# Left operands made five products ahead, and a row of 1/rms spread one product sooner, in a hybrid decoder layer

## The chip, the cores and the metric

The kernel runs on one core of a Trainium2 chip. The metric is the time of one execution on the device in microseconds; the median of three runs is taken. TensorE does the matrix products (PE in the profile, its weight loads PEld), VectorE (DVE) the elementwise work on two inputs, ScalarE (ACT) copies and functions of one input, GpSimd (POOL) here little but issuing the DMAs that add to what lies at their target, and SyncE (SP) issues the plain DMAs.

## The reference, cut to what matters

One decoder layer on 1024 positions of width 1024, in float32:

```python
h = rms_norm(x, g_mix)
va, ga, xb, gb, sa, sb = split(h @ w_in + b_in)
y_a = silu(layer_norm(conv31(va * sigmoid(ga)))) @ w_a_out
y_b = (rg_lru(conv4(xb)) * gelu(gb)) @ w_b_out
x   = x + (sigmoid(sa) * y_a + sigmoid(sb) * y_b) @ w_o     # x1 below
h   = rms_norm(x, g_mlp)
x   = x + square(relu(h @ w_1)) @ w_2                       # up and down products
out = rms_norm(x, g_final)
```

The change lies at the passage from the product with `w_o`, which makes x1, over the norm of x1 to the first products with `w_1`.

## The kernel before

**Products in two parts.** Each float32 operand is split into a high part, rounded to the fast matmul format, and a low part, the rest; a product is then high*high + high*low + low*high. The high part is a copy on ScalarE. The low part is made either on VectorE (`low`, line 1062: source minus high part) or with a DMA (`split_dma`, lines 63 to 67): ScalarE writes the negated, rounded source (line 65), GpSimd issues a DMA that adds the source to it (line 66), and ScalarE writes the high part (line 67). Which sign is kept where does not matter here: a product of this kind can run its first two matmuls as soon as line 67 is done, and its third only once that DMA has landed.

**Blocks of seven products.** The products with `w_a_out` ("a"), `w_o` ("o") and `w_1` ("u") are cut two by two and done with seven block products in place of eight. One block product is twelve matmuls of 128x128 by 128x512 (`g_mm`, line 1266; `up_mm`, line 1544), four pieces of the inner dimension by three pairs of parts. The sequence of these products is a list, `gseq` (line 1197): 28 for "a", 28 for "o", and then eight of "u", the block products 1 and 2 of the first four pairs of output blocks. So index 51 is the last of the four "o" products number 5, 52 to 55 are the four "o" products number 3, 56 to 59 are ("u", 0 to 3, 1) and 60 to 63 are ("u", 0 to 3, 2). In the profile the results of "o" are called go0a, go3e and the like, by pair and bank, and those of "u" gu0a to gu3a. The rest of the products with `w_1` follow in a second list, `useq` (line 1717), with results f0b, f0c, f0d and so on; its left operands are made by `up_lhs` (line 1510) and are called o, from sums and differences s of the raw weights.

**The order is written by hand.** The order on every engine in this part is the program's. The loop over `gseq` does, for each step n: the work after product n-1 (`g_post`), the twelve matmuls of product n, the left operand of a product further on (`g_lhs`, line 1249), the sums that a still later operand needs, and then a list of extra steps from a table `GX`:

```python
for n in range(len(gseq) + 1):                                  # 1701
    ...
    g_get(n - 1, g_post)                                        # 1703
    if n == o0 + 22:
        x1_root(0)                                              # 1705
    ...
    g_get(n, g_mm)                                              # 1711
    g_get(n + 4, g_lhs)                                         # 1712
    g_get(n + 5, g_sums)
    for f, *a in GX.get(n, ()):                                 # 1714
        f(*a)
```

`o0` is 28, so the entry 22 of the second table is step 50. `u0` is 56. For "u", `g_lhs` always goes by `split_dma`, with the raw weights (`raws`, in the profile w_raw) as source; they are loaded by `up_load` (line 1500) in steps 44 to 50. In the profile the operand of a "u" product in `gseq` is called gu as well, and its split shows as ACT L65 and ACT L67 with gu<-w_raw and its DMA as POOL L66 gu<-w_raw.

**The norm of x1.** The positions are kept in two halves, even and odd tokens. For the even ones: squares and their sums by column (steps 42 to 49), the root (`x1_root`, line 1434), four diagonal blocks with 1/rms on the diagonal, made in turn by VectorE and ScalarE (`x1_diag`, lines 1453 and 1455, tile rdm), and four matmuls with a block of ones, which spread 1/rms over all partitions (`x1_spread`, line 1458, tile rbm):

```python
def x1_spread(o):                                               # 1458
    rd, rbk[o] = rbk[o], bank(f"rbm{o}")
    for i in range(4):
        d = slice(i * P, (i + 1) * P)
        nc.tensor.matmul(rbk[o][:, d], ones, rd[:, d], start=True, stop=True)
```

Then VectorE scales x1 (`x1_normed`, line 1468), and `g_parts` (line 1208) makes the two parts of the right operands: gu1h and gu1l for block product 1, gu2h and gu2l for number 2. The even tokens' 1/rms is spread in step 51, behind product 51. For the odd tokens the transposition on TensorE, the squares of the eight transposed banks on ScalarE (`x1_rows`, line 1404, squares at line 1418) and the root stand in step 56, the diagonal blocks in step 57 and the spread in step 58. Before that, `x1_turn` (line 1385) writes the even tokens' x1 to memory with sixteen DMAs on SyncE's queue, ahead of two more loads of raw weights.

The result banks in PSUM are eight, the large SBUF tiles 37 (`T`, line 44), handed out in the order in which they become free.

Of the kernel before, what the change touches and what calls it, by code (L numbers as in the profile page):

```python
# [30 lines left out]
def trunk_kernel(ctx: ExitStack, tc: tile.TileContext, x, xt_in, xt_eo, vecs, w_in, w_a_out, w_b_out,  # L31
# [668 lines left out]
    def vector_work(end):  # L700
        for ready, _, cost, f, a in sorted(todo, key=lambda x: x[:2]):
            dve(cost, ready, f, *a)
        todo.clear()
        taps["wait"] += fresh
        fresh.clear()
        fill(end)
# [77 lines left out]
    for i in range(2, NZ):  # L784
        n = zseq.index((i, 1))
# [281 lines left out]
    def b_load(j):  # L1067
        for n in range(2):
            braw[j, n] = W(f"wb{j}{n}_raw", "raw").rearrange("p (k c) -> p k c", c=P)
            nc.sync.dma_start(braw[j, n], w_b_out[j, n])  # L1070

    def b_parts(j):
        bw[j] = []
        for n in range(2):
            raw = braw.pop((j, n))
            h, l = (W(f"wb{j}{n}_{x}", "w" + x, F32R).rearrange("p (k c) -> p k c", c=P) for x in "hl")
            nc.scalar.activation(h, raw, AF.Copy)
            later(at("A", 0.8), 0.92, low, l, raw, h)
            bw[j] += [(h[:, k, :], l[:, k, :]) for k in range(6)]

    def b_gate(j):
        for hf in range(2):
            sb[j, hf] = EV(f"sb{j}{hf}").rearrange("p (o n) -> p o n", o=2)
            nc.sync.dma_start(sb[j, hf], halved(spill[1, j], hf))

    def b_mm(j):
        bps[j] = ps = [bank(f"yb{j}{hf}") for hf in range(2)]
        ops = [(w, wl, *hg[k]) for k, (w, wl) in enumerate(bw.pop(j))]
        if j < 7:
            todo = [x for w, wl, h, l in ops for x in ((w, h), (w, l))]  # L1090
            todo += [(wl, h) for w, wl, h, l in ops]
        else:

            todo = [x for w, wl, h, l in ops for x in ((w, h), (w, l), (wl, h))]
        for n, (a, b) in enumerate(todo):
            for hf in range(2):
                nc.tensor.matmul(ps[hf], a, b[:, HALVES[hf]], start=n == 0, stop=n == len(todo) - 1)  # L1097
        at("P", 72 * MM)

    def b_out(j):  # L1100
        ps = bps.pop(j)
        for hf in range(2):
            def mult(g, src, j, hf):
                tt(g, src.rearrange("p (n o) -> p o n", o=2), g, ALU.mult)
                nc.sync.dma_start(halved(mbd[j], hf), g)

            later(0, 0.63, mult, sb.pop((j, hf)), ps[hf], j, hf)
# [4 lines left out]
    def n_load():  # L1112
        for o in range(2):
            for kk in range(2):
                for c2 in range(2):
                    q[kk, o, c2] = a = T(f"q{kk}{o}{c2}")
                    for i in range(2):
                        nc.sync.dma_start(a[:, HALVES[i]], yd[4 * kk + 2 * c2 + i, :, HALVES[o]])
# [23 lines left out]
    def n_mean():  # L1142
        for o in range(2):
            mean[o] = n_sum(ysum[0][:, HALVES[o]], f"mu{o}")

    def n_center(o):
        held = []

        def add(s):
            tt(vacc[o], vacc[o], s, ALU.add)  # L1150

        for kk, c2, i in n_pieces(o):
            a = q[kk, o, c2][:, HALVES[i]]
            dve(0.63, 0, tt, a, a, mean[o], ALU.subtract)
            s = EV(f"sq{o}{kk}{c2}{i}")
            if o not in vacc:
                vacc[o] = s
                nc.scalar.activation(s, a, AF.Square)
                at("A", 0.62, clk["V"])
                continue  # L1160
            nc.scalar.activation(s, a, AF.Square)
            ready = at("A", 0.62, clk["V"])
            if held:
                dve(0.63, held[0][0], add, held.pop(0)[1])
            held.append((ready, s))
        dve(0.63, held[0][0], add, held[0][1])

    def n_var(o):
        rstd[o] = n_sum(vacc[o], f"var{o}")

    def n_root(o):
        pv = rstd[o]
        v, s, r = EV(f"lv{o}"), EV(f"lsd{o}"), EV(f"lr{o}")
        nc.vector.tensor_scalar(v, pv, EPS, None, ALU.add)
        newton_rstd(r, v, s, s)
        at("V", 7.5)
        at("A", 1.9)
        rstd[o] = r

    def n_scale(kk, o):  # L1180
        for c2 in range(2):
            for i in range(2):
                a, j = q[kk, o, c2][:, HALVES[i]], 4 * kk + 2 * c2 + i
                dve(0.63, 0, tt, a, a, rstd[o], ALU.mult)
                nc.scalar.activation(a, a, AF.Silu, scale=lng_c[:, j:j + 1], bias=lnb_c[:, j:j + 1])
                at("A", 0.62, clk["V"])
# [10 lines left out]
    gseq = [(w, i, p) for w in "ao" for p in GORD for i in range(GP)]  # L1197
# [10 lines left out]
    def g_parts(w, p, c2):  # L1208
        src = g_src(w, p, c2)
        gh[w, p, c2] = h = T(f"g{w}{p}h{c2}", F32R)  # L1210
        gl[w, p, c2] = l = T(f"g{w}{p}l{c2}", F32R)
        if w == "u" and p == 2:
            split_dma(src, h, l)
            at("A", 2.0)
            return
        nc.scalar.activation(h, src, AF.Copy)
        later(at("A", 1.0), 1.2, low, l, src, h)
# [12 lines left out]
    def g_load(w, i, kk):  # L1230
        graw[w, i, kk] = raw = T(f"w{w}{i}_{kk}").rearrange("p (m k c) -> p m k c", m=2, c=P)
        nc.sync.dma_start(raw, g_left[w][2 * i:2 * i + 2, :, 4 * kk:4 * kk + 4, :].rearrange(
            "m p k c -> p m k c"))
# [377 lines left out]
    def g_get(n, f):  # L1611
        return f(*gseq[n]) if 0 <= n < len(gseq) else None
# [23 lines left out]
        19: ((x1_add,), (x1_sq, 2, 1), (up_load, 3, (0,))),  # L1636
        20: ((x1_add,), (x1_sq, 3, 1), (flush,), (x1_turn, 0)),
        21: ((x1_add,), (flush,), (x1_cols,), (x1_turn, 1), (up_load, 0, (1,))),
        22: ((x1_diag, 0), (up_load, 1, (1,))),
        23: ((x1_spread, 0), (x1_normed, 0, 0)), 24: ((g_parts, "u", 1, 0), (g_parts, "u", 1, 1)),  # L1640
        25: ((x1_normed, 1, 0),), 26: ((g_parts, "u", 2, 0),), 27: ((g_parts, "u", 2, 1),)}.items()})
    u0 = 2 * o0
    GX.update({u0 + n: v for n, v in {
# [6 lines left out]
    with tc.manual_schedule(engines=ENGINES):  # L1650
        for j in range(8):
            clk["A"], clk["V"] = max(clk["A"], clk["P"] + 0.5), max(clk["V"], clk["P"] - 2)
            if j == 0:
                b_load(1)
                b_gate(0)
                n_load()
            if j == 2:
                n_mean()
            if j == 4:
                n_var(0)  # L1660
                n_var(1)
            if j:
                b_out(j - 1)
            b_gate(j + 1) if j < 7 else None
            b_mm(j)
            if j < 7:
                b_parts(j + 1)
            if j < 6:
                b_load(j + 2)
            vector_work(clk["V"])  # L1670
            if j < 2:
                vector_work(math.inf if j else clk["P"] - 0.3)
            elif j < 4:
                n_center(j - 2)
            elif j == 4:
                n_root(0)
                n_root(1)
            elif j == 5:
                for b in (0, 1, 3, 2):
                    n_scale(b % 2, b // 2)  # L1680
            elif j == 6:
                g_parts("a", 1, 0)
                g_parts("a", 1, 1)
                g_load("a", 0, 0)
                g_load("a", 1, 0)
            else:
                g_load("a", 2, 0)
                g_get(0, g_lhs)
                g_load("a", 3, 0)
                g_get(1, g_lhs)  # L1690
                g_t("a", 0, 1, 2)
                g_t("a", 1, 1, 2)
                g_parts("a", 2, 0)
                g_get(2, g_lhs)
                g_parts("a", 2, 1)
                g_load("a", 0, 1)
                g_get(3, g_lhs)
                g_load("a", 1, 1)
            vector_work(clk["V"])
        b_out(7)  # L1700
        for n in range(len(gseq) + 1):
            clk["A"], clk["V"] = max(clk["A"], clk["P"] + 0.5), max(clk["V"], clk["P"] - 2)
            g_get(n - 1, g_post)
            if n == o0 + 22:
                x1_root(0)
            if n > o0:
                vector_work(clk["V"])
                if n == u0:
                    to_mlp()
            g_get(n + 3, g_gate)  # L1710
            g_get(n, g_mm)
            g_get(n + 4, g_lhs)
            g_get(n + 5, g_sums)
            for f, *a in GX.get(n, ()):
                f(*a)
            vector_work(clk["P"] - 0.3)
# [382 lines left out]
```

## Time and profile before

| what | value |
|---|---|
| median of 3 runs | 1544.23 us (1544.19 to 1544.71) |
| profiled execution | 1544.64 us, its span 1542.9 us |
| TensorE busy | 1533.1 us, 99% of the span, 6782 instructions |
| VectorE busy | 1222.5 us (79%) |
| ScalarE busy | 903.6 us (59%) |
| GpSimd busy | 184.4 us (12%) |
| granted TensorE clock | 0.999 |
| DMA | 307.82 MB, 200 GB/s on average |

The profile is of one execution. Times in it count from the start of the span. A row of a timeline gives the start, the duration, the engine, the line, the operation, the tiles (out<-in, without their numbers), how many instructions were merged into the row, and in brackets the idle time just before and what ended it. Matmuls overlap: a duration of 0.39 goes with a start every 0.227. In the rows of DMA issues the last number is the time from issue to landing in microseconds. The shares of the queues q0 (GpSimd's DMAs) and q1 (SyncE's) are of all 16 DMA engines in the window asked for.

### The profile page before, as it was taken

What the parts mean: (1) busy time and instruction counts of PE and PEld (TensorE: products, weight loads), DVE (VectorE), ACT (ScalarE), POOL (GpSimd) and SP (SyncE); (2) the same over time, 40 slices, a digit from 0 to 9 for tenths busy, and PEclk for the clock granted to TensorE, in tenths of its full rate; (3) what the DMA queues carried; (4) which work ended last, traced back from release to release, by engine and by line L of the source; (5) the groups of instructions that cost most, each with busy time, mean ns of one, the idle gap of its engine ahead of it and who ended that gap; (6) DMA issues with size and microseconds to landing.
All of it is one profiled execution on the core that took longest, in us unless ns stands there. A gap on an engine that the chain in (4) does not pass through costs nothing.

```text
span 1542.9 us, 19178 instructions
## 1 busy us (share of the span) xinstructions
PE 1533.1 (99%) x6782; PEld 1262.4 (82%) x6782; DVE 1222.5 (79%) x1648; ACT 903.6 (59%) x1261; POOL 184.4 (12%) x219
## 2 busy tenths in 40 slices
PE   9999999999999999999999999999999999999998
PEld 8888788888888888888888887888888888888886
DVE  6899999979899997478569879755555558888897
ACT  6648576567567667345275777554444475555553
POOL 0000000002222222000022332000000001111110
PEclk9999999999999999999999999999999999999999
DMA  8776978898997879953579898333333779888862
GB/s 347 197 189 161 251 187 222 217 280 217 247 253 196 193 191 246 327 157 116 182 201 299 197 193 204 137 122 112 113 114 111 241 216 228 223 222 224 209 130 110
DMA packets 132288, 307.82 MB, mean 200 GB/s; under 512 B 13232, under 2 KB 35248, under 8 KB 132192
## 3 DMA queue, kind: packets, MB, share of 16 engines
q1 hardware_dynamic: 101744, 230.60, 46.0%
q0 software_dynamic: 30304, 75.74, 26.9%
q8 instruction: 53, 0.87, 0.2%
q14 instruction: 43, 0.35, 0.1%
q10 hardware_dynamic: 144, 0.26, 0.0%
HBM read 147.69 MB, written 58.72 MB: 134 GB/s over the span
## 4 chain that ended last, share of the span: by engine, by line
PE 95%; DMA 2%; issue 1%; DVE 1%; SPq 0%; POOL 0%; ACT 0%; POOLq 0%; DVEq 0%
PE z L726 18%; PE d L1863 15%; PE yb L1097 8%; PE e L1983 3%; PE keep L1863 2%; PE z L258 1%; PE rg L534 1%; PE rg L536 1%; PE rg L535 1%; DMA x<-in_x_dram 1%; DMA gu<-w_raw 1%; DMA xc<-in_xt_dram 0%; PE go3f L1274 0%; PE f15d L1550 0%; PE f15c L1550 0%
## 5 line engine op out<-in xcount | busy, mean ns | idle before, releaser
L726 PE MATMUL z<-xh,win_h 128*128 128x512 f32 x400 | 124.9, 390 | 0.0
L726 PE MATMUL z<-xl,win_h 128*128 128x512 f32 x400 | 124.5, 389 | 0.0
L1875 DVE TENSOR_TENSOR acc<-acc,d 128x1024 f32<-128x1024 f32 x72 | 87.8, 1219 | 33.3 <-PE d L1863 32.6
L726 PE MATMUL z<-xh,win_l 128*128 128x512 f32 x400 | 98.2, 391 | 0.0
L726 PEld LDWEIGHTS z<-xh,win_l 128*128 128x128 f32 x400 | 75.1, 188 | 16.9
L726 PEld LDWEIGHTS z<-xh,win_h 128*128 128x128 f32 x400 | 75.0, 188 | 16.7 <-ACT win_h L67 0.7
L637 DVE SCALAR_TENSOR_TENSOR y<-u,vec,y 128x511 f32<-128x511 f32 (+14 forms) x120 | 88.3, 736 | 0.0
L726 PEld LDWEIGHTS z<-xl,win_h 128*128 128x128 f32 x400 | 75.1, 188 | 15.8
L542 ACT ACTIVATE g<-rg,vec 96x1024 f32<-96x1024 f32 x32 | 35.6, 1113 | 85.5 <-issue 46.0
L637 DVE SCALAR_TENSOR_TENSOR y<-yt,csum,y 128x511 f32<-128x511 f32 (+6 forms) x112 | 82.5, 736 | 0.0
L637 DVE SCALAR_TENSOR_TENSOR yt<-u,vec,yt 128x511 f32<-128x511 f32 (+6 forms) x112 | 82.5, 736 | 0.0
L66 POOL DMA_DIRECT2D win_l<-win_raw x25 | 21.8, 871 | 324.3 <-ACT win_l L65 312.3
L1538 ACT ACTIVATE o<-s 128x512 fp32r<-128x512 f32 x56 | 33.7, 623 | 45.7 <-DVE s L1522 26.4
L66 POOL DMA_DIRECT2D zo<-zw x42 | 36.6, 871 | 129.4 <-ACT zo L65 116.1
L1097 PE MATMUL yb<-hgl,wb_h 128*128 128x512 f32 x168 | 51.7, 389 | 0.0
L1097 PE MATMUL yb<-hgh,wb_h 128*128 128x512 f32 x168 | 51.7, 389 | 0.0
L486 DVE SCALAR_TENSOR_TENSOR v<-xb,vec,v 128x1023 f32<-128x1023 f32 (+2 forms) x36 | 46.2, 1282 | 6.9 <-ACT v L477 6.1
L66 POOL DMA_DIRECT2D db_1l<-wr x7 | 6.1, 870 | 310.5 <-ACT db_1l L65 287.9
L1097 PE MATMUL yb<-hgh,wb_l 128*128 128x512 f32 x168 | 41.0, 389 | 0.0
L65 ACT ACTIVATE zo<-zw 128x512 fp32r<-128x512 f32 x42 | 26.3, 625 | 20.7 <-PE z10f L914 2.1
L1063 DVE TENSOR_TENSOR o<-s,o 128x512 fp32r<-128x512 f32 x56 | 37.3, 683 | 0.5 <-ACT o L1538 0.5
L1097 PEld LDWEIGHTS yb<-hgh,wb_h 128*128 128x128 f32 x168 | 31.5, 188 | 6.6
(1805 smaller groups left out, 4669.7 us busy)
## 6 DMA issues: line engine op xcount, KB each, us to landing
w_raw<-in_w_dram SPq DMA_DIRECT2D x34, 512.0 KB, 5.7
fr<-fd SPq DMA_DIRECT2D x32, 512.0 KB, 6.3
wr<-in_w_dram SPq DMA_DIRECT2D x32, 512.0 KB, 6.6
zw<-in_w_in_dram SPq DMA_DIRECT2D x28, 512.0 KB, 6.3
win_raw<-in_w_in_dram SPq DMA_DIRECT2D x25, 512.0 KB, 6.8
win_l<-win_raw POOLq DMA_DIRECT2D x25, 512.0 KB, 6.7
zo<-zw POOLq DMA_DIRECT2D x42, 256.0 KB, 5.6
gates<-zg SPq DMA_DIRECT2D x32, 256.0 KB, 3.9
```

What stands on the lines that cost most here:

```text
L65: nc.scalar.activation(l, src, AF.Copy, scale=-1.0)
L66: nc.gpsimd.dma_start(l, src, accum_op=ALU.add)
L486: nc.vector.scalar_tensor_tensor(v[:, d:S], a[:, 0:S - d], cbw_c[:, w * 12 + t:w * 12 + t + 1], v[:, d:S], ALU.mult, ALU.add)
L542: nc.scalar.activation(a, gps.pop((n, gi))[:HD, :], AF.Sigmoid, bias=(ba_c, bx_c)[gi][:, n:n + 1])
L637: nc.vector.scalar_tensor_tensor(o[:, k:], a[:, 0:HS - k], c, o[:, k:], ALU.mult, add)
L726: nc.tensor.matmul(zps[s][:, HALVES[hf]], w[:, k, :], xw[k][part][hf], start=n == 0, stop=n == 23)
L1063: tt(l, src, h.bitcast(F32), ALU.subtract)
L1097: nc.tensor.matmul(ps[hf], a, b[:, HALVES[hf]], start=n == 0, stop=n == len(todo) - 1)
L1538: nc.scalar.activation(o[:, 0], src, AF.Copy)
L1863: nc.tensor.matmul(o, a, b, start=n == 0 and (p != 1 or g == 0), stop=n == len(todo) - 1, skip_group_check=p == 1 and g > 0)
L1875: tt(acc[p, q2], acc[p, q2], ps, ALU.add)
L1983: nc.tensor.matmul(o, a, b, start=n == 0 and t not in LOADED, stop=n == len(todo) - 1, skip_group_check=t in LOADED)
```

## The change

Two things are moved; no instruction is added or taken away.

The left operands of the eight "u" products in `gseq` are made five products ahead, where those of all others are still made four ahead. In step 51 two operands are made, those of products 55 and 56; from then on step n makes that of product n+5, and step 59 makes none. Since the call stands ahead of the table's extra steps, the operand of product 61, for one, now is split in step 56 ahead of `up_lhs` and `x1_rows`, in place of step 57 behind them; that of 57 is split in step 52 ahead of `g_parts` of gu1.

The four matmuls that spread the even tokens' 1/rms stand in step 50, behind product 50 and directly behind `x1_diag`, in place of step 51, behind product 51. The scaling of x1 that reads them stays in the table of step 51.

```diff
-        22: ((x1_diag, 0), (up_load, 1, (1,))),
-        23: ((x1_spread, 0), (x1_normed, 0, 0)), 24: ((g_parts, "u", 1, 0), (g_parts, "u", 1, 1)),
+        22: ((x1_diag, 0), (x1_spread, 0), (up_load, 1, (1,))),
+        23: ((x1_normed, 0, 0),), 24: ((g_parts, "u", 1, 0), (g_parts, "u", 1, 1)),
...
             g_get(n, g_mm)
-            g_get(n + 4, g_lhs)
+
+            for d in (4, 5):
+                if n + d < len(gseq) and (gseq[n + d][0] == "u") == (d == 5):
+                    g_get(n + d, g_lhs)
             g_get(n + 5, g_sums)
```

## The prediction

> **What bounds the kernel now.** I read the page first, then the waits of TensorE, then the timelines of all engines around the one wait that the change can touch, and last the DMA view, one issue at a time, for the time from issue to landing.
>
> ```profile
> span 1542.9 us, 19178 instructions
> ...
> PE 95%; DMA 2%; issue 1%; DVE 1%; SPq 0%; POOL 0%; ACT 0%; POOLq 0%; DVEq 0%
> ...
> PE gu1a L1274 <- DMA gu<-w_raw: 1.7, 1, 1.7
> ```
>
> The chain that ended last is matmul for 95% of the span, and between the start-up and the end the waits view holds one wait of TensorE: the second half product of pair 1 (gu1a) waits once for a DMA. So the kernel is a row of matmuls, and whatever does not move a matmul is free. All else that the change does has to be read by one question: which transfer or vector result does TensorE meet late, or just in time?
>
> ```profile
> 932.95 0.39 PE L1274 MATMUL gu1a<-gu2h,gu 128*128 128x512 f32 x1
> 933.17 0.39 PE L1274 MATMUL gu1a<-gu2l,gu 128*128 128x512 f32 x1
> 935.23 0.74 PE L1274 MATMUL gu1a<-gu2h,gu 128*128 128x512 f32 x2 [1.67 <-DMA gu<-w_raw]
> ...
> 937.67 0.39 PE L1274 MATMUL gu2a<-gu2h,gu 128*128 128x512 f32 x1
> ```
>
> The first two matmuls need the high part of the left operand, the third its low part, which an accumulating DMA makes. Matmuls start 0.227 apart where nothing waits (932.95 to 933.17), so twelve take 2.72; this product takes 937.67 - 932.95 = 4.72. The stall costs 2.00 us, of which 0.16 is slow restart beyond the late start (935.23 against 933.40 is 1.83).
>
> **Why that transfer is late.** ScalarE, which writes the high part and the negated source (lines 65 and 67), GpSimd, which issues the accumulate, and the landing times of three transfers in the order of the queue:
>
> ```profile
> 916.64 0.61 ACT L65 ACTIVATE gu<-w_raw 128x512 fp32r<-128x512 f32 x1
> ...
> 917.68 0.62 ACT L65 ACTIVATE o<-s 128x512 fp32r<-128x512 f32 x1
> ...
> 918.72 0.57 ACT L1418 ACTIVATE sq<-tr 128x512 f32<-128x512 f32 x1
> ...
> 924.45 0.62 ACT L65 ACTIVATE gu<-w_raw 128x512 fp32r<-128x512 f32 x1
> ...
> 917.55 0.87 POOL L66 DMA_DIRECT2D gu<-w_raw  x1 [0.60 <-ACT gu L65]
> 918.59 0.87 POOL L66 DMA_DIRECT2D o<-s  x1 [0.17 <-issue]
> 925.36 0.94 POOL L66 DMA_DIRECT2D gu<-w_raw  x1 [5.90 <-ACT gu L65]
> ...
> gu<-w_raw POOLq DMA_DIRECT2D x1, 256.0 KB, 12.4
> o<-s POOLq DMA_DIRECT2D x1, 256.0 KB, 14.0
> gu<-w_raw POOLq DMA_DIRECT2D x1, 256.0 KB, 9.8
> ```
>
> In step 56 ScalarE splits the operand of product 60 (916.64), then that of product 64 (o, 917.68), then squares eight transposed banks from 918.72 on, and only in step 57, at 924.45, comes to product 61. Its DMA goes out at 925.36 and lands 9.8 later, at 935.2: that is the stall.
>
> **The change, part by part.**
>
> *Operands five ahead.* For products 56 to 63 the split moves one step earlier; step 51 does two. Nothing is added or taken away: eight pairs of ScalarE copies and eight accumulates, as before. Product 61 moves from step 57 to step 56 and so ahead of the squares: its DMA goes out before the o transfer, no later than 918.6 instead of 925.36. A pessimistic landing: it takes the place in the queue that o has now, 918.59 + 14.0 = 932.6. Needed at 933.40. The stall goes: **-2.00**. Products 62 and 63 take the ScalarE places of 61 and 62. Without the stall the low part of 62 is read 2.00 sooner than now, at 937.67 + 0.45 - 2.00 = 936.1; in 61's present place it lands, with 61's own time, at 925.36 + 9.8 = 935.2. That holds with 0.9 to spare. On ScalarE product 57 lands in front of the high parts of gu1, where the engine is idle:
>
> ```profile
> 905.68 1.06 ACT L1216 ACTIVATE gu1h<-x 128x1024 fp32r<-128x1024 f32 x1 [2.56 <-issue]
> ```
>
> One pair costs about 1.04 (two copies, 0.52 from start to start: 916.64 to 917.68 is the pair), and 2.56 covers it. Without that cover gu1's high part would come 1 us later, at some 908, and products 52 to 55, four times 2.72, still lie ahead of its first reader. On GpSimd the accumulates move ahead of those of gu2 only; SyncE's own order is untouched.
>
> *The spread one product sooner.* Four small matmuls move from behind product 51 to behind product 50, so TensorE, which takes them in order, now meets them while their input is being made. The first product queued behind them, go3e, and everything after it waits with them.
>
> ```profile
> 900.38 0.39 PE L1274 MATMUL go3e<-go5h,go 128*128 128x512 f32 x1
> ...
> 903.10 1.05 PE L1463 MATMUL rbm<-rdm,ones 128*128 128x128 f32 x8
> 903.91 0.48 PE L1274 MATMUL go0e<-go3h,go 128*128 128x512 f32 x1
> ...
> 900.35 0.70 ACT L1455 ACTIVATE rdm<-ident,stm 128x128 f32<-128x128 f32 x2 [0.29 <-DVE stm L105]
> ...
> 900.29 0.48 DVE L1453 TENSOR_SCALAR rdm<-ident,stm 128x128 f32<-128x128 f32 x2
> ```
>
> The spread would start at 900.38 and take 0.81 (903.10 to 903.91), 0.2 for each of its four blocks. The blocks come in turn from VectorE and ScalarE, the last one at 900.35 + 0.70 = 901.05. If each matmul waits for its own block alone, the last is due at 900.99 and loses 0.06; if all wait for the last, 0.7. The first block is half of VectorE's pair, at about 900.55, so I take **+0.4**. A gain is excluded, since the matmuls are the same. What it gives VectorE (the scaling of x1 some 2 us sooner) moves nothing that TensorE waits for.
>
> *What is late next.* So far -1.6. After this point TensorE runs 1.6 us sooner against VectorE and ScalarE, whose own chains do not start sooner. The tightest meeting that follows is in f1d, product (1,7):
>
> ```profile
> 948.17 0.87 POOL L66 DMA_DIRECT2D o<-s  x1 [0.80 <-ACT o L65]
> ...
> o<-s POOLq DMA_DIRECT2D x1, 256.0 KB, 8.2
> ...
> 957.17 0.62 PE L1550 MATMUL f1d<-gu7h,o 128*128 128x512 f32 x2
> ...
> 947.24 0.63 ACT L65 ACTIVATE o<-s 128x512 fp32r<-128x512 f32 x1
> ...
> 946.51 0.69 DVE L1526 TENSOR_TENSOR s<-w_raw,w_raw 128x512 f32<-128x512 f32 x1
> ...
> 927.67 5.35 DVE L462 SCALAR_TENSOR_TENSOR x<-x,vec,rbm 128x512 f32<-128x512 f32 x8
> ```
>
> The low part lands at 948.17 + 8.2 = 956.4 and is read at 957.17: 0.8 to spare. Its source s is done on VectorE at 946.51 + 0.69 = 947.20 and split at 947.24, and VectorE works without a break worth naming from the second scaling at 927.67, behind the odd tokens' spread, up to there. So this transfer does not follow TensorE forward; the 0.4 of the early spread even pushes it back a little (I take 0.15, between 0 and 0.4). Read time falls to 955.6, landing is 956.5: a new wait of 0.95, and with the 0.16 of slow restart **+1.1**. (f0d, one product before, waits for its own part of it; that shortens the wait in f1d and adds nothing.) The next to come has more room:
>
> ```profile
> 950.16 0.87 POOL L66 DMA_DIRECT2D o<-s  x1 [1.12 <-ACT o L65]
> ...
> o<-s POOLq DMA_DIRECT2D x1, 256.0 KB, 8.0
> ```
>
> It lands at 958.2 and is read twelve matmuls after 957.17, at 959.89: 1.7 to spare, more than is left of the gain by then.
>
> Sum: -2.0 + 0.4 + 1.1 = **-0.5 us**. The profiled execution took 1544.64 (its span and 1.74 around it), so 1544.1 for such a run; the median of the runs is 0.41 lower, which makes 1543.7.
>
> A rule to weigh: the Trainium skill (DMA: Bandwidth & Descriptors, section "Anatomy of one DMA — SWDGE (gpsimd) path") fits one such transfer with 2.0 us and its bytes over 436 GB/s, which is an estimate of 2.6 us for 256 KB. The rows above (8.2 to 14.0) do not agree, and the measurement decides; by the page there would be neither the old stall nor the new wait, and the change would be worth +0.4.
>
> **The rivals.**
>
> *All of the gain stays.* The new wait stands on 8.2 us for one transfer. One of the same size and kind, three issues earlier in the same queue, has this row:
>
> ```profile
> o<-s POOLq DMA_DIRECT2D x1, 256.0 KB, 3.3
> ```
>
> If the transfers around 948 shift against the weight loads beside them so that this one takes 6 to 7, only -2.0 + 0.4 = -1.6 remains: 1542.6. Against it: its issue is tied to VectorE and the loads beside it keep their places.
>
> *The transfer is early but lands no sooner.* The DMA engines are loaded through all of this stretch; if product 61's part is overtaken by the row writes of x1 all the same, the stall stays, swallows the 0.4, and nothing changes: 1544.2. Against it: even o's present place in the queue is early enough.
>
> *Slower: the moved accumulates hold up a weight load.* Products 57 to 59 now put their transfers out near 904 to 908, beside SyncE's writes of x1 and ahead of the loads at 909.11.
>
> ```profile
> 909.11 1.71 SPq L1505 DMA_DIRECT2D w_raw<-in_w_dram  x2
> ...
> w_raw<-in_w_dram SPq DMA_DIRECT2D x1, 512.0 KB, 5.9
> w_raw<-in_w_dram SPq DMA_DIRECT2D x1, 512.0 KB, 9.4
> ...
> 915.11 0.69 DVE L462 TENSOR_TENSOR x<-xe,go3e 128x512 f32<-128x512 f32 x1 [0.90 <-PE go3e L1274]
> 915.71 0.69 DVE L1521 TENSOR_TENSOR s<-w_raw 128x512 f32<-128x512 f32 x1
> ...
> q1 hardware_dynamic: 557, 0.27, 52.1%
> ...
> q1 hardware_dynamic: 321, 0.35, 91.5%
> ```
>
> The last two rows are 908 to 910 and 910 to 912: in the second the accumulates' queue is almost empty and SyncE's gets 91.5% of the engines instead of 52.1%. Filling that gap takes this share away. The first load lands at 909.11 + 5.9 = 915.0, VectorE takes it at 915.71 (at 916.1 with the 0.4), behind it stand o's split, the squares, the odd tokens' spread and VectorE's long chain to f1d. So 1.1 us is free; what is beyond goes into that chain. If the first load took the 9.4 of the second, it would be 3.5 late, the chain 2.4 late instead of 0.15, and the sum -0.5 + 2.2 = +1.7: 1545.9. It decides from about 1.8 us of delay on.
>
> The Trainium skill (DMA: Bandwidth & Descriptors, section "Queues, rings and completion order") says that each DMA engine takes its queues in turn, packet by packet; the two shares agree with it, and it is the reason to give this rival weight.
>
> **How the numbers follow.** Two runs differ by some 0.5 us (1544.19 to 1544.71); 0.2% is 3.1 us and about what a measurement of this kernel can tell from no change. Forecast, the stall traded for a shorter one in f1d (1543.7): 0.55. All gain kept (1542.6): 0.2. Nothing moved (1544.2): 0.08. The load held up (1545 to 1546): 0.17. The range takes in the second case and the first half of the last: 1542.6 to 1545.3. Faster by over 0.2% would need more than the only stall there is: 0.01. Slower by over 0.2% would need a delay of 5 us in that load, or buffers handed out in another order that bring a stall I cannot see from here: 0.04. Within: 0.95.
>
> **What would show it.** Right: no wait of gu1a for gu<-w_raw; the accumulate of product 61 issued before 919; the first spread starting at 900.4 to 901 with a gap of 0.1 to 0.7 before go3e; and a wait of f0d or f1d for o<-s of about 1 us in all. Wrong: f0d and f1d without a wait (all gain kept), gu1a or gu2a still waiting (the queue, not the issue, decides), or the odd tokens' spread waiting for its blocks with w_raw landing after 916.5 (the slower rival).

## The result, and the profile after

The changed kernel is slower: 1550.73 us median of five runs (1549.31 to 1550.84), against 1544.23 us (1543.59 to 1544.93) of the kernel before on the same chip. The ratio is 1.0039, 95% interval 1.0024 to 1.0054. The forecast was 1543.7 us with a range up to 1545.3, so it was wrong, and on the wrong side.

The profiled execution of after took 1550.05 us. Two lines of its page, the span and the chain that ended last:

```profile
span 1548.3 us, 19179 instructions
...
PE 94%; DMA 2%; issue 2%; DVE 1%; POOL 1%; SPq 0%; ACT 0%; POOLq 0%; DVEq 0%; ACTq 0%
```

Then the waits of TensorE (us in total, times, longest):

```profile
PE tr L1413 <- DVE x1r L1422: 4.3, 1, 4.3
...
PE f0d L1550 <- DMA o<-s: 0.3, 1, 0.3
```

The kernel is still a row of matmuls. The wait of gu1a for gu<-w_raw is gone, as forecast. In its place the transposes of the odd tokens (tr) wait 4.3 us, once, for VectorE. The rows left out are of the start-up.

Now the timelines of ScalarE, VectorE and TensorE around that wait, of after:

```profile
907.19 0.63 ACT L65 ACTIVATE gu<-w_raw 128x512 fp32r<-128x512 f32 x1 [0.95 <-DMA x1d<-x1r]
...
916.24 0.63 ACT L65 ACTIVATE gu<-w_raw 128x512 fp32r<-128x512 f32 x1 [7.89 <-DMA x1d<-x1r]
...
923.16 0.61 ACT L65 ACTIVATE o<-s 128x512 fp32r<-128x512 f32 x1
...
924.20 0.57 ACT L1418 ACTIVATE sq<-tr 128x512 f32<-128x512 f32 x1
...
918.99 0.69 DVE L1521 TENSOR_TENSOR s<-w_raw 128x512 f32<-128x512 f32 x1 [2.66 <-DMA w_raw<-in_w_dram]
...
924.90 3.68 DVE L1422 COPY x1r<-tr 128x512 f32<-128x512 f32 x6 [4.49 <-ACT sq L1418]
...
918.16 3.22 PE L1413 MATMUL tr<-ident,x 128*128 128x128 f32 x28
925.65 0.66 PE L1413 MATMUL tr<-ident,x 128*128 128x128 f32 x4 [4.27 <-DVE x1r L1422]
926.24 0.60 PE L1274 MATMUL gu1a<-gu1h,gu 128*128 128x512 f32 x1
926.64 0.63 PE L1274 MATMUL gu1a<-gu1l,gu 128*128 128x512 f32 x1
...
930.69 0.39 PE L1274 MATMUL gu2a<-gu1h,gu 128*128 128x512 f32 x1
```

Read it from the bottom up. 28 of the 32 transposes run; the last four have no PSUM bank, because VectorE has not yet copied one out. VectorE's copies (L1422) wait for ScalarE's squares, which start at 924.20; in before they started at 918.72. The squares stand in ScalarE's queue behind everything else, and ScalarE lost 7.89 us at 916.24: the split of product 59's operand waits for a write of x1 to memory (x1d<-x1r). The tile that this split fills had been given the SBUF buffer of the last turned piece of x1, and SyncE's DMA was still reading from it. In before the same buffer went to the operand of product 60, at 916.64, and the write had landed by then. (The trace leaves buffer numbers out; which tile takes over which buffer stands in the program as built.) So one product further ahead, plus an order of hand-outs shifted by one, put ScalarE in front of a buffer that was not free. The wait of 0.95 at 907.19 is the same thing one piece of x1 earlier: product 58's operand has the buffer of the last but one.

The DMA view of after, the issues between 905 and 917 (KB each, median us from issue to landing):

```profile
w_raw<-in_w_dram SPq DMA_DIRECT2D x2, 512.0 KB, 9.5
gu<-w_raw POOLq DMA_DIRECT2D x2, 256.0 KB, 8.0
x1d<-x1r SPq DMA_DIRECT2D x3, 128.0 KB, 8.7
```

The same issues in before:

```profile
w_raw<-in_w_dram SPq DMA_DIRECT2D x2, 512.0 KB, 7.7
...
x1d<-x1r SPq DMA_DIRECT2D x3, 128.0 KB, 6.4
```

The last write of x1 alone, first its issue on SyncE's queue and its landing in after, then its landing in before:

```profile
907.46 1.68 SPq L1394 DMA_DIRECT2D x1d<-x1r  x1
...
x1d<-x1r SPq DMA_DIRECT2D x1, 128.0 KB, 8.7
...
x1d<-x1r SPq DMA_DIRECT2D x1, 128.0 KB, 6.1
```

And the shares of the queues in after, for 908 to 910 and, the last row, 910 to 912 (in before SyncE's q1 had 52.1% and 91.5%):

```profile
q0 software_dynamic: 172, 0.31, 92.4%
q1 hardware_dynamic: 134, 0.06, 15.9%
...
q1 hardware_dynamic: 454, 0.22, 46.0%
```

The accumulates of products 57 and 58, issued at 904.26 and 908.12 in place of 909.02 and behind it, took SyncE's share of the DMA engines, as the slower rival said: 15.9% and 46.0% are left. (That of product 59 went out only at 917.16, behind the wait.) The writes of x1 land after 8.7 us in place of 6.4. The last one, at 907.46 + 8.7 = 916.2, is what ends ScalarE's wait. But the late landing is the smaller part of that wait: ScalarE wanted the buffer at 916.24 - 7.89 = 908.35, and with the 6.1 us of before it would have come free at 913.6, so an estimated 5.2 of the 7.89 us come from the order of the hand-outs alone. The weight load, issued behind the writes, is late too: VectorE waits 2.66 us for it at 918.99. In this trace that holds up nothing: the sum is done at 920.4, and ScalarE comes to its split at 923.16.

One more view, the stretches of TensorE in after with the clock granted (the column after the busy time):

```profile
921.40:925.60 4.20, 0.00 (x0) 1.00 1.08 194
...
926.20:930.60 4.40, 4.40 (x13) 0.61 1.07 234
```

After the idle 4.2 us TensorE gets a mean of 0.61 of its clock for the next 4.4 us. Matmuls that start 0.227 apart elsewhere start 0.40 apart here (926.24 to 926.64), and the twelve of gu1a take 4.45 in place of 2.82. The stall is thus paid nearly one and a half times.

**The sum of the two traces.** The eight matmuls of the column sums, before anything of the change, in before:

```profile
L1400 PE MATMUL cs<-ones,sq x8: 164/250/250, 896.7 to 897.4; 128*128 128x1 f32 x8
```

and in after (start of the first and of the last):

```profile
L1400 PE MATMUL cs<-ones,sq x8: 164/250/250, 896.9 to 897.6; 128*128 128x1 f32 x8
```

And TensorE's timeline of before at the places named below:

```profile
917.63 3.65 PE L1413 MATMUL tr<-ident,x 128*128 128x128 f32 x32
921.04 0.48 PE L1274 MATMUL gu1a<-gu1h,gu 128*128 128x512 f32 x1
...
923.86 0.39 PE L1274 MATMUL gu2a<-gu1h,gu 128*128 128x512 f32 x1
...
959.43 0.39 PE L1550 MATMUL f0c<-gu3h,o 128*128 128x512 f32 x1
```

After comes into the passage 0.2 later, before anything of the change. Up to the transposes it loses 0.3 more (918.16 against 917.63, less that 0.2), which is the early spread. From there to the start of gu2a it takes 930.69 - 918.16 = 12.53 where before took 923.86 - 917.63 = 6.23: 6.30 lost, of which 4.27 is the wait, 1.63 the slow clock (gu1a takes 4.45 in place of 2.82) and 0.40 the restart around it. From gu2a to f0c (964.85 in after) it gains 1.41: the 2.00 of the old stall less 0.6 that f0d and its neighbours give back. 0.2 + 0.3 + 6.3 - 1.4 = 5.4, the difference of the spans (1548.3 - 1542.9). The medians differ by 6.5; the profiled run of after was one of its faster ones, that of before lies 0.4 above its median.

### The profile page after: what moved, and what is told of

Read it like the earlier page. It is cut to its first block, busy times and chain, and to the rows that moved or that the text cites. A ratio compares the mean times of both kernels' runs of the same rounds, so it can differ in the third digit from the quotient of the medians.

```text
span 1548.3 us, 19179 instructions
## 1 busy us (share of the span) xinstructions
PE 1534.6 (99%) x6782; PEld 1262.0 (82%) x6782; DVE 1223.1 (79%) x1648; ACT 903.6 (58%) x1261; POOL 184.8 (12%) x219
## 4 chain that ended last, share of the span: by engine, by line
PE 94%; DMA 2%; issue 2%; DVE 1%; POOL 1%; SPq 0%; ACT 0%; POOLq 0%; DVEq 0%; ACTq 0%
PE z L726 18%; PE d L1866 15%; PE yb L1097 8%; PE e L1986 3%; PE keep L1866 2%; PE z L258 1%; PE rg L534 1%; PE rg L536 1%; PE rg L535 1%; DMA x<-in_x_dram 1%; DMA x1d<-x1r 1%; DMA o<-s 0%; DMA xc<-in_xt_dram 0%; PE go3f L1274 0%; PE f1d L1550 0%
## 5 line engine op out<-in xcount | busy, mean ns | idle before, releaser
L1097 PEld LDWEIGHTS yb<-hgl,wb_h 128*128 128x128 f32 x168 | 31.5, 188 | 6.6
```

## The experiments

Two theories stood after this reading. *Buffer*: the wait for the buffer of x1 is the whole cost. *Sharing*: what the moved accumulates take from SyncE's queue is the cost, through the writes of x1 and through the weight load, and the buffer is only where it shows. The early spread had to be priced by itself. The ratios below are to the kernel before as measured again beside each group: 1544.12 for the first four kernels, 1544.02 for the four with early loads that follow, 1543.96 for the last four.

**The two halves alone.** First the spread one product sooner with the operands four ahead as before:

```diff
-            for d in (4, 5):
-                if n + d < len(gseq) and (gseq[n + d][0] == "u") == (d == 5):
-                    g_get(n + d, g_lhs)
+            g_get(n + 4, g_lhs)
```

> The spread one product sooner alone, the operands four ahead as before. Theory of the early spread alone: it costs 0.5 us on TensorE (its wait for the diagonal blocks), which the old stall of gu1a swallows, so 1544.2 to 1544.7 and squares at line 1418 starting at 918.7 as before. Buffer theory: with the spread moved, the buffers of the turned x1 (x1r) are handed out again two to four operands sooner; here gu2l0, not the operand of product 59, gets the last of them. ScalarE then waits at line 65 for gu2l until that write lands, about 913.3 in place of a start at 909.8, its queue runs 1.5 us behind the old one, the squares start near 920.2, and the time is 1545.5 to 1546.5, with no w_raw later than 915.5. Sharing theory (moved accumulates slow the weight load): nothing was moved there, so 1544.2.

Measured: 1548.52 us, ratio 1.0028 (1.0016 to 1.0039). The buffer theory's direction and its wait were right, the size not (1545.5 to 1546.5 were expected). ScalarE's timeline:

```profile
915.32 1.06 ACT L65 ACTIVATE gu2l<-x 128x1024 fp32r<-128x1024 f32 x1 [7.07 <-DMA x1d<-x1r]
```

TensorE's wait in it:

```profile
PE tr L1413 <- DVE x1r L1422: 2.0, 1, 2.0
```

And two stretches of TensorE, with the granted clock, as above:

```profile
923.50:926.00 2.50, 2.31 (x9) 0.72 1.06 188
926.00:930.00 4.00, 4.00 (x15) 0.75 1.07 318
```

This "small" half makes the same kind of stall with no operand moved by the program: the early spread brings x1's parts to ScalarE sooner, so ScalarE splits products 57 and 58 at 906.07 and 907.11 in place of 907.96 and 909.00, and the buffer that is not free is this time that of gu2's low part. Gu1a's old stall is gone here too, though product 61's operand is where it was: TensorE now comes to gu1a late enough.

Then the operands five ahead, with the spread where it was:

```diff
-        22: ((x1_diag, 0), (x1_spread, 0), (up_load, 1, (1,))),
-        23: ((x1_normed, 0, 0),), ...
+        22: ((x1_diag, 0), (up_load, 1, (1,))),
+        23: ((x1_spread, 0), (x1_normed, 0, 0)), ...
```

> The left operands five ahead alone, the spread behind product 51 as before. Buffer theory: the last x1r buffer goes to gu2h1, which is wanted only near 915, so ScalarE never waits more than about 1 us for it and the 7.9 us wait of the changed kernel is gone. Sharing theory: the accumulates of products 57 and 58 still go out at 904 to 908, w_raw still lands near 918.5 to 919 in place of 915.0, VectorE waits for it about 2.5 us, the squares start near 921.3, and the time is 1545.5 to 1546.5. If the buffers are all of the cause and sharing costs nothing: 1542.9 to 1543.7. If the operands five ahead alone are the cause in some other way: 1550.

Measured: 1546.67 us, ratio 1.0017 (1.0008 to 1.0026). The sharing theory's range is missed by 0.2. The runs spread from 1545.03 to 1550.76, more than those of any other kernel here, and the profile is of the fastest, so what the slower ones met is not seen. In the profiled one no split waits for a write; the weight load is late and the chain behind it too:

```profile
918.17 0.69 DVE L1521 TENSOR_TENSOR s<-w_raw 128x512 f32<-128x512 f32 x1 [1.94 <-DMA w_raw<-in_w_dram]
...
919.62 0.63 ACT L65 ACTIVATE o<-s 128x512 fp32r<-128x512 f32 x1 [1.41 <-DVE s L1522]
```

So neither half is free, and their costs (4.4 and 2.6 by the medians) add up to about the whole, 6.5, though not by the same waits.

**The buffers kept out of the way.** The changed kernel, in which a one-column read of each turned piece of x1 in step 57 keeps their four buffers from being handed on before that (the reads add four tiny copies on ScalarE; lines behind 1384 move by 8):

```diff
+    turned = []
+
+    def x1_hold():
+        for r in turned:
+            nc.scalar.activation(warm[:, 4:5], r[:, 0:1], AF.Copy)
+        turned.clear()
...
             r = T(f"x1r{kk}{th}")
+            turned.append(r)
...
-        1: ((x1_diag, 1),), 2: ...
+        1: ((x1_diag, 1), (x1_hold,)), 2: ...
```

> The changed kernel with both parts, but the four x1r buffers are kept: ScalarE reads one column of each into a scrap column in step 57, so none of them is handed out before. Four more ScalarE instructions of about 0.2 us behind the odd diagonal blocks; nothing is left out. Buffer theory: the 7.9 us wait of ScalarE before gu<-w_raw is gone, and with it most of the 6.5 us. What is left is sharing: w_raw near 919, squares near 921.3, 1545.5 to 1546.8. Sharing theory alone: the squares still start near 924 and the time stays at 1549 to 1551.

Measured: 1548.54 us, ratio 1.0031 (1.0018 to 1.0043). Only 2.2 of the 6.5 us came back: the time lies between the two theories' ranges (1545.5 to 1546.8, 1549 to 1551), and the buffer as the whole cost is out. The timelines of VectorE, ScalarE and TensorE:

```profile
920.13 0.69 DVE L1529 TENSOR_TENSOR s<-w_raw 128x512 f32<-128x512 f32 x1 [3.70 <-DMA w_raw<-in_w_dram]
...
921.59 0.63 ACT L65 ACTIVATE o<-s 128x512 fp32r<-128x512 f32 x1 [4.01 <-DVE s L1530]
...
924.09 0.66 PE L1421 MATMUL tr<-ident,x 128*128 128x128 f32 x4 [2.59 <-DVE x1r L1430]
```

The 7.9 us wait is gone. ScalarE now sends product 59's accumulate out at 908 in place of 917, a fourth transfer ahead of the weight load, and the load lands still later (920.1 against 919.0). VectorE's sum s waits for it, ScalarE's split of o waits for s, and the squares stand behind that split. The two causes take each other's place: while the first holds ScalarE, it keeps back the transfer that would make the second worse.

**Only the operands that need it.** Products 60 to 63 five ahead, 56 to 59 four, the spread where it was:

```diff
-                if n + d < len(gseq) and (gseq[n + d][0] == "u") == (d == 5):
+                if n + d < len(gseq) and (gseq[n + d][0] == "u" and gseq[n + d][2] == 2) == (d == 5):
```

> Only the operands of products 60 to 63 five ahead (step 55 makes two), those of 56 to 59 four ahead, the spread as before. No accumulate goes out before 909, so by the sharing theory w_raw lands at 915 to 915.5 as before; by the buffer theory the last x1r buffer goes to gu2h1 at 915.7, after its write has landed, and nothing waits. ScalarE has one pair more (1.04 us) ahead of the squares, which start near 919.7; the stall of gu1a goes (-2.0), and 1.0 comes back at the odd spread and about as much at f1d: 1543.9 to 1544.9. If the first half of the change is harmful in itself, whatever the buffers and the load: above 1546.

Measured: 1544.64 us, ratio 1.0003 (0.9994 to 1.0012), within what was expected. No transfer is added in front of the weight load, and VectorE waits for it only briefly:

```profile
916.94 0.69 DVE L1521 TENSOR_TENSOR s<-w_raw 128x512 f32<-128x512 f32 x1 [0.79 <-DMA w_raw<-in_w_dram]
```

The harm of the operands is therefore in moving 57 to 59, not in splitting 61 earlier. But the 2.0 us of the old stall, which is gone here, did not show as a gain either. The trace says where they went: from the first transpose to gu2a TensorE loses 0.8 (6.23 became 7.03; the transposes wait 0.4 and it restarts slowly), and from f0d to the f0c behind f1d another 0.8 (5.44 became 6.27).

**The weight loads taken out of the crowd.** The crowd here is the accumulates and the writes of x1 that share the DMA engines from about 904 to 917. Two loads are issued in step 48, ahead of the writes of x1, in place of steps 49 and 50 behind most of them:

```diff
-        20: (..., (flush,), (x1_turn, 0)),
-        21: (..., (x1_turn, 1), (up_load, 0, (1,))),
-        22: (..., (up_load, 1, (1,))),
+        20: (..., (flush,), (up_load, 0, (1,)), (up_load, 1, (1,)), (x1_turn, 0)),
+        21: (..., (x1_turn, 1)),
+        22: (...),
```

This was done to four kernels: to the one with the buffers kept,

> As e3_hold, and the two loads of raw weights that the operands o of the first two pairs need stand ahead of the sixteen writes of x1 in SyncE's queue (step 48) in place of behind them. Against e3_hold only these loads move. Sharing theory (what e3_hold had left, 4.4 us, is the weight load that lands at 920 and VectorE's wait of 3.7 for it): the load lands before 905, that wait is gone, the squares start near 919.0, and the time falls to 1543.3 to 1544.8. If the four kept buffers or the early spread make the rest of the loss: it stays at 1547 to 1548.5.

to the changed kernel,

> The changed kernel as it is, without the kept buffers, and the same two loads ahead of the writes of x1. Besides the load, the buffers fall differently: the last x1r buffer goes to a row tile of the odd tokens, the last but one to a square, neither wanted before 918. Both causes gone, by buffer and sharing theory together: no wait of ScalarE for x1d, squares near 918.8, the gain of the stall less the wait in f1d as first forecast, 1543.0 to 1544.3. If the early spread has a cost of its own that comes through: 1544.3 to 1545.5.

to the one with the operands five ahead alone,

> Operands five ahead without the early spread, and the two loads ahead of the writes. Sharing theory: VectorE's wait of 1.9 for w_raw that e2_ahead had is gone, squares near 918.8, no wait of gu1a, about 1 us of waits in f0d and f1d: 1542.8 to 1544.0. If the load were not what cost e2_ahead 2.5 us: 1546 to 1547.

and, as the control, to the kernel before.

> Control: the kernel before with only the two loads moved ahead of the writes of x1. Product 61 is still split behind the squares, so gu1a still waits for its accumulate (about 1.7 us) and the time stays within 0.5 us of before: 1543.7 to 1544.7. If the load alone is worth something, the squares would start before 918.5 and the time fall below 1543.5.

Measured, in this order: 1544.70 (ratio 1.0003, 0.9994 to 1.0013), 1544.99 (1.0007, 0.9998 to 1.0016), 1544.26 (0.9997, 0.9988 to 1.0006) and 1543.86 us (1.0001, 0.9992 to 1.0010). With the buffers kept, the place of the two loads is the only edit between 1548.54 and 1544.70: the late weight load is worth 3.8 us there. The control shows that the place of the loads brings the kernel before nothing that can be measured, so these 3.8 us are the crowd's, not a gain of their own. In the changed kernel the loads alone take back 5.7 of 6.5 us, and not by the load's own lateness: with the loads gone from their old place, the buffers of x1 fall to other tiles as well, and no split waits for one, so that run takes both causes away at once and can't divide them. It lies 0.7 above what was expected of it, and the operands-only version 0.3 above. What the two wait for in the end is f0d's operand; TensorE's timeline of the changed kernel with early loads:

```profile
954.71 0.74 PE L1550 MATMUL f0d<-gu7h,o 128*128 128x512 f32 x2 [1.52 <-DMA o<-s]
```

and of the operands five ahead with early loads:

```profile
953.63 0.73 PE L1550 MATMUL f0d<-gu7h,o 128*128 128x512 f32 x2 [0.34 <-DMA o<-s]
```

That is the wait forecast as the next one. The control's time is as expected, its trace is not: gu1a was expected to wait still, and it does not. Its timelines of GpSimd and TensorE at product 61:

```profile
926.57 0.94 POOL L66 DMA_DIRECT2D gu<-w_raw  x1 [5.90 <-ACT gu L65]
...
934.60 0.62 PE L1274 MATMUL gu1a<-gu2h,gu 128*128 128x512 f32 x2
```

and the issue of 926.57 in its DMA view:

```profile
gu<-w_raw POOLq DMA_DIRECT2D x1, 256.0 KB, 6.1
```

The transfer still goes out behind the squares, but takes 6.1 us in place of 9.8 and lands at 932.7, with 1.9 to spare. The stall that the change was after disappears without the change. In that profile the control comes to the spread's blocks 1.2 later than before did (901.49 against 900.29, though the two are the same up to step 48), so times from the start of two profiles are not compared closer than about 1 us here. What the stall cost in the other runs of before is not seen: had each run of before lost 2.0 to it, the control's median would lie some 1.5 lower (0.5 goes again in f0d and f1d), and it lies 0.2 lower.

**The early spread with the loads early.**

```diff
-        22: ((x1_diag, 0),),
-        23: ((x1_spread, 0), (x1_normed, 0, 0)), ...
+        22: ((x1_diag, 0), (x1_spread, 0)),
+        23: ((x1_normed, 0, 0),), ...
```

> The kernel before with the spread one product sooner and the two weight loads ahead of the writes of x1; operands stay four ahead. The theory (the long wait came from writes of x1 that land late beside the moved accumulates and hold a buffer; the early spread by itself costs only its own wait for the diagonal blocks, 0.5 us): 1544.0 to 1544.8, no wait of ScalarE of over 2 us for a write of x1 ahead of the squares, the spread meeting TensorE near 901 with 0.5 idle. Rival (the early spread alone lets ScalarE and VectorE run into buffers not yet free, loads or not): 1546 to 1548.5, as with the spread alone.

Measured: 1545.32 us, ratio 1.0007 (0.9998 to 1.0017). The rival (1546 to 1548.5) is out: without the crowd the early spread makes no long wait. But it is 0.5 above the theory's range. The trace shows this wait,

```profile
954.75 0.73 PE L1550 MATMUL f0d<-gu7h,o 128*128 128x512 f32 x2 [0.81 <-DMA o<-s]
```

and a wait of 0.5 of TensorE's weight load for the spread's blocks, of which 0.35 reaches the matmuls: from the column sums to the first transpose they take 21.27 in place of the control's 20.93. The pairs with and without the early spread differ by 4.1 (1550.73 against 1546.67), 0.7 (1544.99 against 1544.26) and 1.5 us (1545.32 against 1543.86).

The part beyond the 0.35 has a cause that the section on the change does not have. With the early spread VectorE's order as built is another one: two sums for a later operand (lines 1524 and 1526), which in before come behind the odd tokens' scaling of x1 (at 937.49 and 939.23; the scaling starts at 927.67), stand ahead of it. VectorE's timeline in the changed kernel with early loads:

```profile
927.96 0.68 DVE L1524 TENSOR_TENSOR s<-w_raw,s 128x512 f32<-128x512 f32 x1
928.67 0.69 DVE L1526 TENSOR_TENSOR s<-w_raw,w_raw 128x512 f32<-128x512 f32 x1
929.28 5.35 DVE L462 SCALAR_TENSOR_TENSOR x<-x,vec,rbm 128x512 f32<-128x512 f32 x8
```

and with the operands five ahead and early loads, without the early spread:

```profile
928.50 5.35 DVE L462 SCALAR_TENSOR_TENSOR x<-x,vec,rbm 128x512 f32<-128x512 f32 x8
```

The scaling starts 0.8 later, though the transposes started 0.1 sooner (918.21 against 918.35), and all of VectorE's chain to f0d and f1d follows it. From f0d to the f0c behind f1d TensorE takes 7.30 in place of 6.53 in this pair, and 6.86 in place of 5.97 in the pair with the control. With the 0.35 that makes 1.1 and 1.2 us for the early spread without the crowd. In the two kernels of the next experiment the sums stand behind the scaling with and without the early spread, and they differ by 0.3.

**The next wait taken away.** The changed kernel with early loads, and the operands of (0,7) and (1,7) split right behind those of (0,5) and (1,5):

```diff
-        6: (..., (up_lhs, 0, 5)),
-        7: (..., (up_lhs, 1, 5), (g_t, "u", 0, 3), ...)
+        6: (..., (up_lhs, 0, 5), (up_lhs, 0, 7)),
+        7: (..., (up_lhs, 1, 5), (up_lhs, 1, 7), (g_t, "u", 0, 3), ...)
...
-    ready = 4
+    ready = 6
```

> The kernel after with the two weight loads early, and the operands of products (0,7) and (1,7) split one and two products sooner, behind (0,5) and (1,5). The theory that these two operands are the next bound of this passage (what is late next), and that ScalarE's place for them sets it: f0d and f1d wait no longer for o<-s (1.5 us and 0.3 us with the loads early alone), 1543.0 to 1544.0. Rival (the DMA engines, with weight loads beside them, set the landing, and an earlier issue lands no sooner; or VectorE's parts of gu5 to gu7 come as much later): 1544.5 to 1545.3.

The same with the spread in its old place:

> As the one before, but with the spread in its old place: operands five ahead, weight loads early, operands (0,7) and (1,7) sooner. By the theory all stalls of the passage are gone, about 0.6 us of f0d and f1d beside the 2.0 of gu1a, less what the floor had taken: 1543.2 to 1544.0, below the kernel before. Rival (landing set by the DMA engines): 1544.0 to 1544.6.

Measured: 1545.34 us (1.0008, 0.9999 to 1.0017) and 1545.03 us (1.0008, 0.9998 to 1.0017). Both miss the theory's ranges and lie above the rivals' (by 0.04 and 0.4). The waits of f0d and f1d are gone, and this is in their place in the first (TensorE, then VectorE):

```profile
950.33 0.50 PE L1550 MATMUL f0c<-gu5l,o 128*128 128x512 f32 x1 [1.67 <-DVE gu5l L1063]
...
945.46 0.69 DVE L1524 TENSOR_TENSOR s<-w_raw,s 128x512 f32<-128x512 f32 x1 [1.65 <-DMA o<-s]
```

The sums for (1,7), made sooner, wait 1.65 us on VectorE for an accumulate (o<-s), which reads a buffer of the five that these sums share, and gu5's low part, behind them, comes 1.67 late. VectorE works almost without a break from the odd tokens' scaling to here; with these operands first, something else of it is last. The product that waits changes; the time does not.

**The best combination that the runs pointed to**: only products 60 to 63 five ahead, the spread in its old place, the loads early (the two edits above together).

> Only products 60 to 63 five ahead, spread in its old place, weight loads early. The theory (f0d and f1d are the floor, whichever way the gu1a stall is taken away): 1543.7 to 1544.4, f0d and f1d waiting up to 0.5 for o<-s. Rival (each accumulate that stays in its old place lets the writes of x1 land sooner and frees the chain of VectorE): 1542.6 to 1543.6.

Measured: 1544.76 us, ratio 1.0005 (0.9996 to 1.0014); expected were 1543.7 to 1544.4, so it missed as well, by 0.4. Its profiled run, 1544.35, was the lowest of eleven. No version is faster than the kernel before by more than its interval.

## Why the prediction was wrong, step by step

The step that failed: the sum has no term for what the moved splits meet on ScalarE. The prediction lets product 57 fall into an idle gap, gives 58 and 59 no price, and holds that the early spread moves nothing that TensorE waits for. In place of that nothing, ScalarE stood 7.89 us before a buffer of x1 and TensorE lost 6.3 us behind it; where the buffer is kept out of the way, the late weight load takes its place (1548.54, and 1544.70 with the loads early). Term by term:

*The stall of gu1a.* It is gone in after, as forecast, but after does not show the step right: TensorE comes to gu1a's second half 6.8 us later there (939.78 against 932.95), product 61's accumulate went out at 923.03 and not before 919, and the early spread alone has no stall either. The term of -2.00 was read as a gain that the operand's place alone decides. The control with early loads shows that the DMA engines' load decides it as well.

*The early spread.* Sized about right where it was looked for: +0.4 forecast, 0.35 in the trace of after (0.3 in the sum above). What failed stands one sentence later: "What it gives VectorE (the scaling of x1 some 2 us sooner) moves nothing that TensorE waits for." It moves ScalarE: alone, it cost 4.4 us. And it moves two sums ahead of VectorE's second scaling, 0.8 us in f0d and f1d without the crowd, where 0.15 was taken.

*Product 57 in the idle gap.* The prediction covered its price by ScalarE's idle 2.56 us ahead of gu1's high parts, and asked when gu1's parts are read. It did not ask what products 58 and 59 meet when they come early. They met a buffer still being written out (0.95 and 7.89 us), in the middle of an in-order queue that also carries the squares. "Buffers handed out in another order that bring a stall I cannot see from here" was named, without a place, at a chance of 0.04 that it shared with a delay of the load by 5 us; this is what came. It could have been looked for: the writes of x1 and their landings were in the trace of before, and one question, which tile gets their buffers once the order moves, was not asked.

*The rival "the moved accumulates hold up a weight load".* It got 0.17, and its mechanism is half of what happened. The shares moved as it said (52.1% to 15.9%, 91.5% to 46.0%), the load landed at 919.0 where the point of decision was about 916.8, and VectorE waited 2.66. But in after this wait is hidden behind ScalarE's. It comes out with the buffers kept, and makes 1548.54 there, where the rival was priced at 1545.9. The price, +2.2, left two things out: the same crowd delays the writes of x1, some 2.6 of the 7.89 us; and the loss does not stop at VectorE's chain to f1d, but stalls the transposes by way of the squares and the PSUM banks.

*The restart.* 0.16 us were added behind a stall, from a row with a stall of 1.67. Behind 4.27 it was 1.63 at a clock of 0.61, plus 0.40.

*What is late next.* Right in place (f0d waits more than f1d), too small in size. The changed kernel with early loads shows the sum as it was meant: gu1a's second half takes 2.00 less, the spread costs 0.35, and f0d and f1d together take 1.86 more (952.57 to 959.87 in place of 953.99 to 959.43), where +1.1 was forecast; 0.8 of that is the moved sums. So without the crowd the change would still have been worth nothing: +0.2 by these terms, +1.0 by the medians (1544.99 against 1544.02). The same meeting takes 0.5 to 1.4 us from the other versions without the crowd, and fits their ending between 1543.9 and 1545.3. Moved out of the way, gu5's low part takes its place.

*The weighed rule of one transfer's time* changed nothing: the accumulates took 8.0 us in after too.

## What to carry to other kernels

An operand made earlier takes three things earlier: a place in an engine's in-order queue, a share of the DMA engines, and a buffer. Look for the tile that holds this buffer before it, and for when that tile's last DMA lands, even if the DMA only reads. When a transfer goes out sooner, price what stands behind it in the other queue by the whole chain to the matmuls, and when a wait is removed by an experiment, see whether it was keeping back something worse. Once the first stall of a passage is gone, what it can give is bounded by the slack of the next meeting, here VectorE's chain; the one reordering of that chain that was tried only moved the wait. And compare the order on every engine as built, not only the lines that were edited.

## What the runs showed of the hardware

TensorE's clock falls behind a stall, and not by the stall's length alone. Behind 4.27 us of waiting in after, the twelve matmuls of gu1a took 4.45 us in place of 2.82; behind 2.00 us (the early spread alone) 4.44; behind 2.59 us (the buffers kept) 2.85, at full clock:

```profile
921.40:924.00 2.60, 0.10 (x1) 1.00 1.10 214
...
924.60:927.40 2.80, 2.80 (x14) 1.00 1.10 221
```

The Trainium skill (TensorE: Matmul & The Clock Gate, "Part 1: The HAM clock gate (the "warmup" mystery)") says that TensorE falls to half its clock after about one idle window of 3.4 us and that this window runs free of the kernel's start. Matmuls 0.40 apart in place of 0.227 come near to half the clock. The wait of 2.0 us is shorter than such a window and cost clock all the same, and the one of 2.6 us cost none. A free-running window could tell the two apart only if part of the 3.2 us of transposes ahead of each stall counted as idle too, which was not tried; the cause stays open.

A write from SBUF to memory holds its buffer for as long as it is in flight: the split that takes the buffer over starts at 916.24, when the write issued at 907.46 has landed, 8.7 us for 128 KB beside the accumulates, against 6.1 for the same write in before.
